# Expert weights in a new host layout, and one expert's load moved into the tile of h

## The chip, the core and the metric

The kernel runs on one core of a Trainium2 chip. The core has five engines with queues of their own: TensorE (PE, with its weight loads shown as PEld), VectorE (DVE), ScalarE (ACT), GpSimd (POOL) and SyncE (SP, which here only issues transfers). Sixteen DMA engines move data between the device memory and the on-chip memory (SBUF, 128 partitions). The metric is the device time of one execution in microseconds (us).

## The reference, cut to what matters

Two layers for 256 tokens of 1,024 features: sparse attention, then a mixture of experts, then a gated embedding. The change lies in the mixture of experts, which runs once in each layer:

```python
def hier_moe(xn, w_group, b_group, w_expert, b_expert, w_gate, w_up, w_down):
    g_prob = softmax(xt @ w_group + b_group)                 # 4 groups, one is taken
    e_logits = (xt @ w_expert + b_expert)                    # 8 experts in the taken group
    ...                                                      # the best two, with their weights
    cw = ...                                                 # [token, 32 experts], two entries per token
    hid = silu(einsum('td,edf->tef', xt, w_gate)) * einsum('td,edf->tef', xt, w_up)
    y = einsum('tef,efd->td', hid * cw[:, :, None], w_down)
```

Here xn is the residual h, normed, with the gain ln_ffn; w_gate and w_up are [2 layers, 32 experts, 1024, 128], w_down is [2, 32, 128, 1024], all in float32.

## The kernel before

The program is written as a straight line of operations on tiles. A planner orders each engine's instructions at build time by its own costs and due times, puts the waits in, and keeps a ring of 102 KB per partition for streamed weights beside a few big named tiles (XA, XB, X2, XH, X3, X4, X5) that are used again and again. SP issues its transfers strictly in its order.

In one mixture of experts, `moe(l, ...)`, the steps are these.

- The last part of the attention output is added to h. The tile of h, [128 tokens, 2 halves, 1024], is XH in the first layer and XA in the second.
- For each half t of the tokens, `transposed(t)` transposes h on PE in eight blocks of 128 features, `logits(t, half)` makes the router's logits with `wr`, `split_h(t)` (line 995, ACT) copies h rounded into `h_hi`, `choose(t)` finds group and experts with a row of small DVE instructions, and `rest_h(t)` (line 998, DVE) writes h minus `h_hi` into `h_lo`. All of these read h through `columns(t)`, which takes feature 8p + k as row p of block k, so neighbours in a block lie 8 elements apart.
- `order(t)` counts each token's place in its expert's list of at most 32 slots; line 986 makes the rank, line 976 (`place`) the one-hot matrix `Gs`. `gather_first` (line 1017) and `gather` (line 1064) multiply `h_hi` and `h_lo` with `Gs`, so that each expert's tokens stand in columns; lines 1088 and 1090 bring them to SBUF with the gain.
- Experts are taken four at a time, in groups j = 0 to 7. `gate_up(j)` (line 1225) runs 64 matmuls on four tiles of weights, `down(j)` (lines 1256 to 1263) the second matrix and the sum into the tokens. `hidden(j)` lies between them.
- `load_wgu(j)` loads gate and up of the four experts, each by two transfers of 512 KB with 4 KB per partition. Groups 0 and 3 use four big tiles, the others the ring. The fourth tile is the one that holds h. `load_wd(j)` loads down. The program calls `load_wgu(0)`, `load_wgu(1)`, `load_wd(0)` after the routing, then `load_wgu(j + 2)` and `load_wd(j + 1)` at group j.
- At group 4 `unsplit_h` (line 1003, DVE) puts h together again from `h_hi` and `h_lo`, through `columns(t)`, into the other of the tiles XA and XH. A ninth, gathered expert (`load_extra`, `rows_of`) covers one list that is longer than 32.

The router's constants come once, in `late_constants`, by seven transfers of the POOL queue during the first attention; line 283 multiplies the gain into `wr`.

Of the kernel before, what the change touches and what calls it, by code (L numbers as in the profile page):

```python
# [18 lines left out]
P = 128  # L19
S = 256  # L20
D = 1024
NT = S // P
NK = D // P
H = 16
HD = 64
NE = 32
NG = 4
# [12 lines left out]
def hybrid_kernel(ctx: ExitStack, tc: tile.TileContext, I: dict, out: bass.AP, dbg=None):  # L40
    nc = tc.nc
# [11 lines left out]
    def nm(s):  # L53
        uid[0] += 1
        return f"{s}_{uid[0]}"
# [7 lines left out]
    def bt(tag, shape, dt=F32):  # L63

        return big.tile(shape, dt, tag=tag, name=nm(tag))

    def wt(tag, shape, dt=F32, bufs=None):
        return wk.tile(shape, dt, tag=tag, name=nm(tag), bufs=bufs)
# [41 lines left out]
    hh = [bt("XH", [P, NT, D])]  # L110
# [45 lines left out]
    rows = wt("hT", [P, P])[0:78]  # L156
# [3 lines left out]
    for r0, src in ((48, I["a_k_norm"][0]), (51, I["a_q_norm"]), (52, I["b_q_norm"]), (53, I["k_norm_shared"][None, :])):  # L160
        n = src.shape[0]
# [41 lines left out]
    for c in range(8):  # L203
        for b in range(2):
            v = SLOPE[8 * (c // 4) + 4 * b + c % 4]
# [38 lines left out]
    g_ffn = cp.tile([P, 2, NK], F32, name="g_ffn")  # L244
    wr = cp.tile([P, 2, NK, NE + NG], F32, name="wr")
    rb = cp.tile([P, 2, NE + NG], F32, name="rb")

    def late_constants():
        nc.gpsimd.dma_start(g_ffn, I["ln_ffn"].rearrange("l (p k) -> p l k", k=NK))
        for l in range(2):  # L250
            nc.gpsimd.dma_start(wr[:, l, :, 0:NE], I["moe_w_expert"][l].rearrange("(p k) e -> p k e", k=NK))
            nc.gpsimd.dma_start(wr[:, l, :, NE:NE + NG], I["moe_w_group"][l].rearrange("(p k) e -> p k e", k=NK))
        nc.gpsimd.dma_start(rb[:, :, 0:NE], I["moe_b_expert"].partition_broadcast(P))
        nc.gpsimd.dma_start(rb[:, :, NE:NE + NG], I["moe_b_group"].partition_broadcast(P))


    iota_e = cp.tile([P, NE], F32, name="iota_e")
# [30 lines left out]

    def columns(t):

        return hh[0][:, t, :].rearrange("q (p k) -> q k p", k=NK)

    def inv_rms(t, ss, rstd):
        junk = wt("sq", [P, D], BF16)
# [577 lines left out]
    def moe(l, out_proj_tail, prefetch):  # L872
# [4 lines left out]
        def load_wgu(j):  # L877
            wgus[j] = []
            for i in range(4):
                e = 4 * j + i  # L880
                gu = [I[src][l, e].rearrange("(p k) f -> p k f", k=NK) for src in ("moe_w_gate", "moe_w_up")]
                if j in (0, 3):
                    w = bt((("XB", "XA", "X2", "XH"), ("XB", "X2", "XH", "XA"))[l][i], [P, 2, NK, P])
                else:
                    w = ring.tile([P, 2, NK, P], F32, name=nm("wgu"))
                for x in range(2):
                    nc.sync.dma_start(w[:, x], gu[x])
                wgus[j].append([w[:, :, k, :] for k in range(NK)])

        def load_wd(j):  # L890
# [41 lines left out]
        def transposed(t):  # L932
            ts_ = slice(t * P, (t + 1) * P)
            inv_rms(t, ss, rstd)
            for k0 in range(0, NK, 4):
                pt = pa([P, 4, P])
                for k in range(4):
                    i = nc.tensor.transpose(pt[:, k, :], columns(t)[:, k0 + k, :], ident)
                if k0:
                    c = nc.scalar.copy(hT[:, k0:k0 + 4, ts_], pt)  # L940
                else:
                    nc.vector.tensor_copy(hT[:, k0:k0 + 4, ts_], pt)
            return i, c
# [3 lines left out]
        def logits(t, half):  # L947
            ts_ = slice(t * P, (t + 1) * P)
            if half == 0:
                pls[t] = pa([P, NE + NG])  # L950
            for k in range(4 * half, 4 * half + 4):
                i = nc.tensor.matmul(pls[t], hT[:, k, ts_], wr[:, l, k, :], start=(k == 0), stop=(k == NK - 1))
            if half == 1:
                nc.vector.scalar_tensor_tensor(lg[:, t, 0:NE + NG], pls[t], rstd[:, t:t + 1], rb[:, l, :], ALU.mult,
                                               ALU.add)
            return i
# [68 lines left out]
        add, i = out_proj_tail(1, 1)  # L1025
        with tc.issue_after(i.ins):
            i = logits(0, 0)
        with tc.issue_after(c.ins):
            split_h(0)
        with tc.issue_after(i.ins):  # L1030
            i, c = transposed(1)
        with tc.issue_after(i.ins):
            i = logits(0, 1)
# [4 lines left out]
        with tc.issue_after(i.ins):  # L1038
            for k in range(2):
                i = logits(1, k)  # L1040
        pg.append(pb([P, 2, 256]))
        with tc.issue_after(i.ins):
            i = keep_warm(pg[0], 4)
        with tc.issue_after(i.ins):
            order(0)
            for k0 in (0, 2):
                i = gather_first(0, k0)
        dump(f"h{1 + 3 * l}", hh[0])
        choose(1)
        with tc.issue_after(i.ins):  # L1050
            i = order(1)
        with tc.issue_after(i.ins):
            for k0 in (4, 6):
                i = gather_first(0, k0)
# [107 lines left out]
        stokx = st("stokx", [CAP, 1], bufs=1)  # L1162
        srsx = st("srsx", [CAP, 1], bufs=1)

        def rows_of(src, o):
            rows = I[src].rearrange("l e d f -> (l e d f)").rearrange("(r n) -> r n", n=D)
            nc.gpsimd.memset(o, 0.0)
            nc.gpsimd.indirect_dma_start(out=o, out_offset=None, in_=rows,
                                         in_offset=bass.IndirectOffsetOnAxis(ap=rowi[:, 0:1], axis=0),
                                         bounds_check=2 * NE * P - 1, oob_is_err=False)  # L1170
# [65 lines left out]

        def load_extra():
            wx.append(bt("X2", [P, 2, D]))
            for x, src in enumerate(("moe_w_gate", "moe_w_up")):
                rows_of(src, wx[0][:, x, :])  # L1240
            wx.append(bt("XB", [P, D]))
            rows_of("moe_w_down", wx[1])

        def hidden(j):
            m = P if j < 8 else CAP
# [35 lines left out]
        def leftover():  # L1281

            cwo = st("oh", [P, NT, NE], bufs=1)
            rs2 = st("rs2", [P, NT], bufs=1)
            nc.vector.tensor_tensor(rs2, rstd, rstd, ALU.mult)
            for t in range(NT):
                nc.vector.tensor_tensor(cwo[:, t], rank[:, t], thr, ALU.is_gt)
            nc.vector.tensor_tensor(cwo, cwo, cw, ALU.mult)
            nc.vector.tensor_tensor(cwo, cwo, rs2[:, :, None].to_broadcast([P, NT, NE]), ALU.mult)
            with tc.For_i(0, rv):  # L1290
                ox = st("ox", [P, 8], bufs=1)
                oi = st("oi", [P, 8], U32, bufs=1)
                nc.vector.max(ox, over)
                nc.vector.max_index(oi, ox, over)
                oif = st("oif", [P, 1], bufs=1)
                nc.vector.tensor_copy(oif, oi[:, 0:1])
                sel = st("sel", [P, NE], bufs=1)
                nc.vector.tensor_scalar(sel, iota_e, oif, None, ALU.is_equal)
                nc.vector.tensor_tensor(over, over, sel, ALU.subtract)
                e = nc.sync.value_load(oi[0:1, 0:1], min_val=0, max_val=NE - 1)  # L1300
                ow = bt("X4", [P, 2, NK, P])
                od = bt("XB", [P, D])
                for x, w in enumerate(("moe_w_gate", "moe_w_up")):
                    nc.sync.dma_start(ow[:, x], I[w][l, bass.ds(e, 1)].rearrange("o (p k) f -> p (o k) f", k=NK))
                nc.sync.dma_start(od, I["moe_w_down"][l, bass.ds(e, 1)].rearrange("o f d -> f (o d)"))
                for t in range(NT):
                    sc_ = st("sc_", [P, NE], bufs=1)
                    cc = st("cc", [P, 1])
                    nc.vector.tensor_tensor(sc_, cwo[:, t], sel, ALU.mult)
                    nc.vector.tensor_reduce(cc, sc_, AX.X, ALU.add)  # L1310
                    gu = banks[0].rearrange("p (x s) -> p x s", x=4)
                    pt = banks[1].rearrange("p (k s) -> p k s", k=4)
                    for k0 in range(0, NK, 4):
                        xT = wt("p1", [P, 4, P], bufs=4)
                        for k in range(4):
                            nc.tensor.transpose(pt[:, k, :], columns(t)[:, k0 + k, :], ident)
                        nc.vector.tensor_tensor(xT, pt, gf[:, k0:k0 + 4, None].to_broadcast([P, 4, P]), ALU.mult)
                        for k in range(4):
                            nc.tensor.matmul(gu[:, 0:2], xT[:, k, :], ow[:, :, k0 + k, :],
                                             start=(k0 + k == 0), stop=(k0 + k == NK - 1))  # L1320
                    hid = silu_mul(gu[:, 0, :], gu[:, 1, :], rstd[:, t:t + 1], cc)
                    nc.tensor.transpose(gu[:, 2, :], hid, ident)
                    hT = wt("hT", [P, P])
                    nc.vector.tensor_copy(hT, gu[:, 2, :])
                    for n in range(2):
                        nc.tensor.matmul(y[t][n], hT, od[:, n * 512:(n + 1) * 512], start=False, stop=False)

        wx = []
# [7 lines left out]
        for j in range(8):  # L1336
# [10 lines left out]
            if j < 7:  # L1347
# [7 lines left out]
                if j in (0, 2, 4):  # L1355
                    i = j // 2 + 1
# [128 lines left out]
    def after_b(c):  # L1485
# [6 lines left out]
    ple(B_p, X)  # L1492


_INS = ['x', 'p', 'ln_mix', 'ln_ffn', 'ln_ple', 'a_w_in', 'a_q_norm', 'a_k_norm', 'a_ck_pos', 'a_ck_w1', 'a_ck_w2',
        'a_cv_pos', 'a_cv_w1', 'a_cv_w2', 'a_w_out', 'kv_norm', 'w_kv_shared', 'k_norm_shared', 'b_w_q', 'b_q_norm',
        'b_w_out', 'moe_w_group', 'moe_b_group', 'moe_w_expert', 'moe_b_expert', 'moe_w_gate', 'moe_w_up',
# [1 line left out]


# [17 lines left out]
```

## Time and profile before

| | us |
|---|---|
| median of 3 runs | 552.87 (551.81 to 553.31) |
| profiled execution | 552.15 |
| its span, first to last instruction | 550.5 |
| PE busy in the span | 523.7 (95%) |
| DVE busy | 351.9 (64%) |
| ACT busy | 282.8 (51%) |
| POOL busy | 57.9 (11%) |

The span is what the trace shows; 1.65 us of the profiled execution lie around it. PE is busy nearly always, so a row that says how long PE stood still and what ended it is worth more here than a row on another engine. [...]

### The profile page before, as it was taken

How to read it: one execution, taken by the hardware profiler on the slowest of the kernel's cores; microseconds unless marked ns; L12 is line 12 of the kernel's file. 1: busy time of each engine (PE TensorE's matmuls, PEld its weight loads, DVE VectorE, ACT ScalarE, POOL GpSimd, SP SyncE). 2: the span in 40 equal slices, each digit the busy share in tenths (PEclk: the TensorE clock that was granted, in tenths of full speed). 3: DMA queues.
4: the chain of work that ended last, by engine and by line, in shares of the span. 5: the costliest groups of instructions: out<-in, count | busy, mean ns of one | idle time of the engine just before them, and what ended most of it. 6: DMA issues, size and time to landing. Idle time of an engine off the chain costs nothing. (4 is left out here: it accounts for less than half of the span.)

```text
span 550.5 us, 10449 instructions
## 1 busy us (share of the span) xinstructions
PE 523.7 (95%) x3804; PEld 373.5 (68%) x3804; DVE 351.9 (64%) x1072; ACT 282.8 (51%) x652; POOL 57.9 (11%) x128
## 2 busy tenths in 40 slices
PE   6999999999897999999999999999987999999996
PEld 6979996677567765464568999656556755555376
DVE  5869979988757645323278986767657535232484
ACT  6759468975526142222379956754352412222391
POOL 5000614213320003100000000000000013000000
PEclk9999999999999899999999999999998999999999
DMA  8986980255778499999972679944672999999702
GB/s 324 356 323 223 189 206 1 86 190 205 299 241 302 176 417 408 391 402 409 387 244 78 208 192 216 405 160 199 224 265 106 402 411 413 410 408 395 272 2 77
DMA packets 52940, 146.14 MB, mean 265 GB/s; under 512 B 5293, under 2 KB 10277, under 8 KB 52885
## 3 DMA queue, kind: packets, MB, share of 16 engines
q1 hardware_dynamic: 51669, 143.38, 72.4%
q0 software_dynamic: 1184, 2.05, 1.4%
q8 instruction: 31, 0.51, 0.4%
q14 instruction: 24, 0.20, 0.1%
q10 hardware_dynamic: 32, 0.01, 0.0%
HBM read 145.94 MB, written 1.05 MB: 267 GB/s over the span
## 5 line engine op out<-in xcount | busy, mean ns | idle before, releaser
L1225 PE MATMUL pb<-wgu,X 128*32 128x256 f32 x768 | 50.4, 380 | 1.0 <-DVE sinf L1150 0.4
L461 ACT ACTIVATE p<-p,mx 128x128 f32<-128x128 f32 (+1 forms) x96 | 42.5, 446 | 9.4 <-DVE mx L459 9.4
L865 ACT ACTIVATE p<-pb,srs 128x128 f32<-128x128 f32 x16 | 5.9, 368 | 80.5 <-PE pb L1225 71.0
L1225 PEld LDWEIGHTS pb<-wgu,X 128*32 128x32 f32 x768 | 29.7, 110 | 17.7 <-issue 2.2
L1270 PE MATMUL pb<-wd,hT 128*32 128x512 f32 x224 | 41.4, 596 | 0.0
L370 DVE TENSOR_TENSOR pta<-pb,p 128x512 fp32r<-128x512 f32 (+1 forms) x36 | 24.8, 690 | 24.0 <-ACT p L370 22.5
L370 ACT CAST p<-pb 128x512 fp32r<-128x512 f32 (+1 forms) x36 | 21.1, 585 | 34.7 <-PE pb L1270 33.2
L381 PE MATMUL pa<-XA,wsp 128*128 128x256 f32 x128 | 37.4, 292 | 0.0
L382 PE MATMUL pa<-XB,wsp 128*128 128x256 f32 x128 | 36.3, 284 | 0.0
L383 PE MATMUL pa<-XA,wsp 128*128 128x256 f32 x128 | 35.9, 282 | 0.0
L868 DVE TENSOR_TENSOR p<-pb,ptb 128x128 f32<-128x128 f32 (+1 forms) x18 | 5.2, 290 | 44.1 <-ACT ptb L867 41.8
L459 DVE CUSTOM_DVE_ANT_0 p<-pb,d_q 128x128 f32<-128x128 f32 (+1 forms) x96 | 29.6, 350 | 4.5 <-PE pb L442 3.4
L490 ACT COPY pta<-pa 128x512 f32<-128x512 f32 (+1 forms) x32 | 14.6, 478 | 34.0 <-PE pa L486 33.8
L472 POOL TENSOR_SCALAR p<-p,cf 128x128 f32<-128x128 f32 x32 | 24.8, 783 | 62.8 <-ACT p L461 29.0
L146 DVE SCALAR_TENSOR_TENSOR wsp<-raw,cols,wsp 128x512 fp32r<-128x512 f32 x40 | 28.0, 747 | 3.4 <-ACT wsp L145 3.3
L571 PE MATMUL pa<-wo,XH 128*128 128x512 f32 x64 | 29.4, 602 | 0.0
L1064 PE MATMUL pb<-rs,X 128*128 128x256 f32 (+1 forms) x192 | 27.1, 293 | 2.0 <-DVE X L1090 2.0
L1064 PEld LDWEIGHTS pb<-rs,X 128*128 128x128 f32 x192 | 24.3, 188 | 5.7 <-DVE X L1090 2.6
L1263 PE MATMUL pa<-p,rrow 128*128 128x512 f32 (+1 forms) x72 | 27.3, 424 | 0.0
L1263 PE MATMUL pa<-pta,rrow 128*128 128x512 f32 (+1 forms) x72 | 26.7, 420 | 0.4 <-DVE pta L370 0.4
L142 DVE SCALAR_TENSOR_TENSOR wsp<-raw,g_mix,wsp 128x256 fp32r<-128x256 f32 x64 | 26.5, 475 | 0.0
L145 ACT ACTIVATE wsp<-raw,cols 128x512 fp32r<-128x512 f32 x40 | 26.2, 717 | 0.0
(385 smaller groups left out, 1464.9 us busy)
## 6 DMA issues: line engine op xcount, KB each, us to landing
wgu<-in_moe_w_gate_dram SPq DMA_DIRECT2D x48, 512.0 KB, 6.5
wgu<-in_moe_w_up_dram SPq DMA_DIRECT2D x48, 512.0 KB, 10.2
wd<-in_moe_w_down_dram SPq DMA_DIRECT2D x48, 512.0 KB, 8.8
raw<-in_a_w_in_dram SPq DMA_DIRECT2D x16, 512.0 KB, 6.0
raw<-in_ple_w_gate_dram SPq DMA_DIRECT2D x16, 512.0 KB, 8.3
wd<-in_moe_w_down_dram SPq DMA_DIRECT2D x16, 256.0 KB, 6.2
wo<-in_a_w_out_dram SPq DMA_DIRECT2D x8, 512.0 KB, 8.4
raw<-in_b_w_q_dram SPq DMA_DIRECT2D x8, 512.0 KB, 4.4
```

The lines of the kernel that those rows point to most:

```text
L146: nc.vector.scalar_tensor_tensor(lo, src, g, hi.bitcast(F32), ALU.mult, ALU.subtract)
L370: return nc.scalar.copy(hi, src), eng.tensor_tensor(lo, src, hi.bitcast(F32), ALU.subtract)
L381: nc.tensor.matmul(o, a[0], b[0], start=first, stop=False)
L382: nc.tensor.matmul(o, a[0], b[1], start=False, stop=False)
L383: return nc.tensor.matmul(o, a[1], b[0], start=False, stop=last)
L459: nc.vector.tensor_tensor_reduce(pt_[:, br, :], st_[:, br, :], dt_, -SLOPE[hh], 3e38, ALU.add, ALU.min, accum_out=mx[:, t, br:br + 1])
L461: mark["exp", c] = nc.scalar.activation(pt_[:, br, :], pt_[:, br, :], AF.Exp, bias=mx[:, t, br:br + 1], scale=-1.0, accum_out=sums[:, t, b ...
L571: m = nc.tensor.matmul(pt, self.oT[0][:, 2 * j + i, t * P:(t + 1) * P], self.raw[j][:, i, n * 512:(n + 1) * 512], start=(i == 0), stop=(i ...
L1064: nc.tensor.matmul(pt, part_columns(x, t)[:, k, :], Gs[i][:, t, 0:e1], start=(t == x == 0), stop=(t == x == 1))
L1225: last_ = nc.tensor.matmul(gu[32 * i:32 * i + 32, 0:2], xg[:, k, 32 * i:32 * i + 32], wgu[i][k], start=(k == 0), stop=(k == NK - 1), tile_ ...
L1263: nc.tensor.matmul(y[t][n], gt[0:m, t * P:(t + 1) * P], ysx[x][0:m], start=(first and x == 0), stop=(final and x == 1))
L1270: nc.tensor.matmul(ysp[32 * i:32 * i + 32, :], hT[:, 32 * i:32 * i + 32], wd[i][n], start=True, stop=True, tile_position=(0, 32 * i))
```

## The change

The host now lays out four inputs before the launch. Gate and up of an expert become one array in which a partition holds its 2 x 8 x 128 values in one run of 8 KB; the order of the features is k * 128 + p for row p of block k. Router weights (experts and groups in one array), router bias and the gain ln_ffn follow the same order. `columns(t)` therefore reads and writes 128 neighbours. A transfer of 1 MB takes the place of two of 512 KB, and three POOL transfers the place of seven. The gathered ninth expert needs one indirect transfer for gate and up where it had two. And in `load_wgu` the fourth expert of group 0 goes to the ring, while the fourth expert of group 1 takes the tile of h.

```diff
 def late_constants():
-    nc.gpsimd.dma_start(g_ffn, I["ln_ffn"].rearrange("l (p k) -> p l k", k=NK))
-    for l in range(2):
-        nc.gpsimd.dma_start(wr[:, l, :, 0:NE], I["moe_w_expert"][l].rearrange("(p k) e -> p k e", k=NK))
-        nc.gpsimd.dma_start(wr[:, l, :, NE:NE + NG], I["moe_w_group"][l].rearrange("(p k) e -> p k e", k=NK))
-    nc.gpsimd.dma_start(rb[:, :, 0:NE], I["moe_b_expert"].partition_broadcast(P))
-    nc.gpsimd.dma_start(rb[:, :, NE:NE + NG], I["moe_b_group"].partition_broadcast(P))
+    nc.gpsimd.dma_start(g_ffn, I["g_ffn"])
+    nc.gpsimd.dma_start(wr, I["router"])
+    nc.gpsimd.dma_start(rb, I["router_b"].partition_broadcast(P))
...
-    return hh[0][:, t, :].rearrange("q (p k) -> q k p", k=NK)
+    return hh[0][:, t, :].rearrange("q (k p) -> q k p", k=NK)
...
             e = 4 * j + i
-            gu = [I[src][l, e].rearrange("(p k) f -> p k f", k=NK) for src in ("moe_w_gate", "moe_w_up")]
-            if j in (0, 3):
+            if j == 3 or (j == 0 and i < 3) or (j == 1 and i == 3):
                 w = bt((("XB", "XA", "X2", "XH"), ("XB", "X2", "XH", "XA"))[l][i], [P, 2, NK, P])
             else:
                 w = ring.tile([P, 2, NK, P], F32, name=nm("wgu"))
-            for x in range(2):
-                nc.sync.dma_start(w[:, x], gu[x])
+            nc.sync.dma_start(w, I["moe_gu"][l, e])
...
-        for x, src in enumerate(("moe_w_gate", "moe_w_up")):
-            rows_of(src, wx[0][:, x, :])
+        rows_of(I["moe_gu"].rearrange("l e p x k f -> (l e p) (x k f)"), wx[0].rearrange("p x d -> p (x d)"))
...
+def _layout(inputs):
...
+    def parts(w):
+        w = w.reshape(*w.shape[:-2], NK, P, w.shape[-1])
+        return np.moveaxis(w, -3, -2)
+    gate, up = a.pop("moe_w_gate"), a.pop("moe_w_up")
+    a["moe_gu"] = np.stack([parts(gate), parts(up)], axis=-3)
+    a["router"] = np.moveaxis(parts(np.concatenate([a.pop("moe_w_expert"), a.pop("moe_w_group")], axis=-1)), 0, 1)
+    a["router_b"] = np.concatenate([a.pop("moe_b_expert"), a.pop("moe_b_group")], axis=-1)
+    a["g_ffn"] = np.moveaxis(a.pop("ln_ffn").reshape(2, NK, P), 2, 0)
```

## Rows read from the trace of the kernel before

**Rows 1.** The page's list of engines: busy us, share of the span, instructions.

```profile
PE 523.7 (95%) x3804; PEld 373.5 (68%) x3804; DVE 351.9 (64%) x1072; ACT 282.8 (51%) x652; POOL 57.9 (11%) x128
```

**Rows 2.** Waits of PE, whole span: us in total, times, longest us.

```profile
PE pb L1017 <- DVE rs L976: 4.7, 2, 2.5
...
PE pb L1064 <- DVE X L1090: 2.0, 3, 0.8
PE pa L485 <- POOL p L472: 1.6, 1, 1.6
PE pb L1225 <- DMA XA<-in_moe_w_up_dram: 1.5, 1, 1.5
PE pb L1017 <- DVE es L1112: 1.4, 2, 0.7
PE pb L1147 <- DVE X L1090: 0.9, 2, 0.5
```

**Rows 3.** Timeline of PE, both layers: start, us, [idle before <- releaser].

```profile
175.90 1.22 PE L1017 MATMUL pb<-rs,X 128*128 128x256 f32 x8 [2.47 <-DVE rs L976]
...
180.36 3.75 PE L1017 MATMUL pb<-rs,X 128*128 128x256 f32 x16 [0.72 <-DVE es L1112]
...
413.23 2.08 PE L1017 MATMUL pb<-rs,X 128*128 128x256 f32 x8 [2.24 <-DVE rs L976]
...
417.76 2.13 PE L1017 MATMUL pb<-rs,X 128*128 128x256 f32 x16 [0.71 <-DVE es L1112]
...
422.00 0.38 PE L1225 MATMUL pb<-XA,X 128*32 128x256 f32 x1 [1.54 <-DMA XA<-in_moe_w_up_dram]
...
426.40 3.78 PE L1225 MATMUL pb<-wgu,X 128*32 128x256 f32 x64 [0.20 <-DVE sinf L1150]
```

**Rows 4.** Timeline of DVE, first layer, routing and group 4.

```profile
173.04 0.26 DVE L954 SCALAR_TENSOR_TENSOR lg<-pa,rstd,rb 128x36 f32<-128x36 f32 x1 [0.27 <-ACT rstd L297]
...
173.29 1.98 DVE L998 TENSOR_TENSOR X<-XH,X 128x1024 fp32r<-128x1024 f32 x1
...
177.56 2.04 DVE L998 TENSOR_TENSOR X<-XH,X 128x1024 fp32r<-128x1024 f32 x1
...
214.65 2.20 DVE L1003 TENSOR_TENSOR XA<-X,X 128x1024 f32<-128x1024 f32 x1 [3.22 <-PE pb L1225]
...
216.88 0.69 DVE L1090 TENSOR_TENSOR X<-pb,g_ffn 128x512 f32<-128x512 f32 x1
...
217.88 2.14 DVE L1003 TENSOR_TENSOR XA<-X,X 128x1024 f32<-128x1024 f32 x1
```

**Rows 5.** Timeline of SP, its transfers: start of issue, us.

```profile
105.47 2.59 SPq L887 DMA_DIRECT2D wgu<-in_moe_w_gate_dram  x2
...
179.75 0.33 SPq L887 DMA_DIRECT2D XH<-in_moe_w_gate_dram  x1
...
187.87 0.34 SPq L887 DMA_DIRECT2D XB<-in_moe_w_gate_dram  x1
...
417.10 0.33 SPq L887 DMA_DIRECT2D XA<-in_moe_w_gate_dram  x1
```

**Rows 6.** Stretches: PE, PEld, DVE, ACT, POOL busy, granted clock, DMA share, GB/s.

```profile
178.00:180.00 2.00, 1.64 (x9) 1.43 (x8) 2.00 (x5) 0.80 (x1) 0.00 (x0) 0.50 0.01 2
...
417.00:418.00 1.00, 0.29 (x4) 0.27 (x3) 1.00 (x7) 0.00 (x0) 0.00 (x0) 1.00 0.00 0
...
188.00:285.00 97.00, 94.24 (x813) 53.80 (x813) 40.55 (x122) 30.30 (x66) 7.42 (x8) 1.00 0.99 385
```

**Rows 7.** Groups by line and shape: busy us, mean ns of one.

```profile
L370 DVE TENSOR_TENSOR wsp<-wo,wsp 128x512 fp32r<-128x512 f32 x16 | 10.8, 696 | 0.0
...
L295 ACT ACTIVATE sq<-XH 128x1024 bf16<-128x1024 f32 x6 | 6.3, 1052 | 3.1 <-DVE XH L574 3.1
...
L868 DVE TENSOR_TENSOR p<-pb,ptb 128x128 f32<-128x128 f32 x16 | 4.7, 292 | 37.3 <-ACT ptb L867 35.0 <-PE pb L1064 2.2
```

**Rows 8.** Timeline of ACT, first layer, the second copy of h.

```profile
170.85 2.05 ACT L995 CAST X<-XH 128x1024 fp32r<-128x1024 f32 x1
```

More of the change, by code (lines that the diff above doesn't have):

```diff
@@ L1163, in moe, with rows_of @@
         srsx = st("srsx", [CAP, 1], bufs=1)
-        def rows_of(src, o):
-            rows = I[src].rearrange("l e d f -> (l e d f)").rearrange("(r n) -> r n", n=D)
+        def rows_of(rows, o):
             nc.gpsimd.memset(o, 0.0)
@@ L1238, in load_extra @@
             wx.append(bt("X2", [P, 2, D]))
-            for x, src in enumerate(("moe_w_gate", "moe_w_up")):
-                rows_of(src, wx[0][:, x, :])
+            rows_of(I["moe_gu"].rearrange("l e p x k f -> (l e p) (x k f)"), wx[0].rearrange("p x d -> p (x d)"))
             wx.append(bt("XB", [P, D]))
-            rows_of("moe_w_down", wx[1])
+            rows_of(I["moe_w_down"].rearrange("l e f d -> (l e f) d"), wx[1])
         def hidden(j):
@@ L1302, in leftover @@
                 od = bt("XB", [P, D])
-                for x, w in enumerate(("moe_w_gate", "moe_w_up")):
-                    nc.sync.dma_start(ow[:, x], I[w][l, bass.ds(e, 1)].rearrange("o (p k) f -> p (o k) f", k=NK))
+                nc.sync.dma_start(ow.rearrange("p x k f -> p (x k f)"),
+                                  I["moe_gu"][l, bass.ds(e, 1)].rearrange("o p x k f -> p (o x k f)"))
                 nc.sync.dma_start(od, I["moe_w_down"][l, bass.ds(e, 1)].rearrange("o f d -> f (o d)"))
@@ L1492, in hybrid_kernel @@
     ple(B_p, X)
+def _layout(inputs):
+    import numpy as np
+    a = {n: np.asarray(inputs[n]) for n in _INS}
+    def parts(w):
[6 more added lines that the diff above has]
+    a["g_ffn"] = np.moveaxis(a.pop("ln_ffn").reshape(2, NK, P), 2, 0)
+    return {n: np.ascontiguousarray(v) for n, v in a.items()}
 _INS = ['x', 'p', 'ln_mix', 'ln_ffn', 'ln_ple', 'a_w_in', 'a_q_norm', 'a_k_norm', 'a_ck_pos', 'a_ck_w1', 'a_ck_w2',
@@ L1501 @@
 def kernel(**inputs):
-    import numpy as _np
     import concourse.bacc as _bacc
@@ L1508 @@
     arrays, aps = {}, {}
-    for name in _INS:
-        a = _np.ascontiguousarray(inputs[name])
+    for name, a in _layout(inputs).items():
         arrays[f"in_{name}_dram"] = a
```

## The prediction, made before the change was run

> **What bounds the kernel now.** I read the list of engines first. PE is busy for 523.7 of 550.5 us and no other engine comes near [rows 1], so time is won only where PE stands still or runs at its low clock. The list of PE's waits comes next [rows 2]. Five of the entries shown lie in the two mixtures of experts, in operations that the change touches: 4.7 and 1.4 us at line 1017 (the first gather waits for the one-hot matrix), 2.0 us at line 1064 and 0.9 us at line 1147 (the third gather waits for line 1090, which empties its PSUM), and 1.5 us at line 1225, the one long wait for a transfer. The timeline of PE tells where these stand [rows 3]: 2.47 and 0.72 us in the first layer's routing, 2.24 and 0.71 us in the second's, and 1.54 us in the second layer's first `gate_up`.
>
> The timeline of DVE gives the reason for the first two kinds [rows 4]. `rest_h` (line 998) takes 1.98 and 2.04 us, and the rank and the one-hot matrix for which PE waits are queued behind it. `unsplit_h` (line 1003) takes 2.20 and 2.14 us, and line 1090 at 216.88 starts just as it ends. Both go through `columns(t)`, 8 elements apart. The transfer is the fourth expert's: its tile is h's own, so SP issues it at 417.10, when `rest_h(1)` has read h [rows 5], and PE gets it at 422.00 [rows 3].
>
> [...]
>
> **The change part by part.** *DVE, a row of 1,024 neighbours.* No such instruction with two inputs is in the trace. The nearest with all operands in SBUF are 512 elements at 0.696 us and 128 at 0.292 us [rows 7]: 1.05 ns an element, so 1.23 us for 1,024. The bounds are 0.70 us (the 512 row) and 1.98 us (no gain at all). I take 1.23, since the line through both rows needs no more than their slope.
>
> *Routing, first layer.* DVE's row from 173.29 to PE's restart at 180.36 has no idle entry of note, so what `rest_h` gives up is given on: 0.75 and 0.81 us. The second copy of h on ACT (2.05 us from 170.85, [rows 8]) stands ahead of the rstd for which DVE waits 0.27 us at 173.04 [rows 4]. A row of 1,024 neighbours on ACT takes 1.05 us [rows 7], a microsecond less, and the 0.27 us go. Together 1.83 us. What is late next is still the chain of small DVE instructions: of the gap of 2.47 us some 1.45 stay.
>
> *Routing, second layer.* The same 0.75 and 0.81 us, with no wait for rstd. Here PE can become the later one: restarted at 412.48, with twice eight matmuls at up to 2.08 us each (the slow ones of 413.23, [rows 3]), it could be free for the last 16 only at 416.64, while DVE would be ready at 416.20. So between 1.1 and 1.56 us; I take 1.4, because the second eight need not all be slow.
>
> *The clock in the first layer.* Between nothing and 3.75 - 2.13 = 1.62 us. In the second layer a standstill of 2.24 us also led to the low clock (eight matmuls in 2.08 us instead of 1.22), but it was back at 1.00 at 417 to 418 [rows 3, 6]. The standstill that stays, 1.45 us, is below both, and nearest to the two of 1.6 and 1.54 us at lines 485 and 1225 [rows 2, 3]; `gate_up` goes on at 422.00 with matmuls of 0.38 us, the full clock's duration. So I take the whole 1.62 us, as the nearest rows have it, and keep nothing as the other end. [...]
>
> *The fourth expert.* In group 0 it goes to the ring, where loads run far ahead (the first at 105.47, [rows 5]); the ring's first eight expert slots stay eight, since group 1 gives one up. The wait of 1.54 us in the second layer goes. In the first layer the same load lands just before its use; it would have become the next wait once the gather is faster, and does not. The load into h's tile is now group 1's. SP can issue it when `rest_h(1)` ends, near 415.5 in the second layer, and as 417.10 to 422.00 was 4.9 us, it lands near 420.4. `gate_up(1)` stands at 426.40 [rows 3] and would come some 4.5 us sooner at most, at 421.9: 1.5 us of cover, and more in the first layer. Group 3's fourth load then waits for `gate_up(1)` instead of `gate_up(0)`. Three transfers of 1 MB are ahead of it, at 385 GB/s [rows 6] 2.7 us each, 8.2 us in all, longer than the 3.78 us of `gate_up(1)` and the gap ahead of it. So the DMA engines don't run dry. What is queued behind it on SP is group 4, for which no slot was free earlier.
>
> *`unsplit_h`.* Line 1064 waits 2.0 us in three times, the longest 0.8; two of 0.8 follow line 1003, and the rest, 0.4, lies elsewhere. Line 1147 waits 0.9 us in two times [rows 2]. With 1.23 us the first `unsplit_h` ends at 215.9, line 868 (0.29 us) follows, and line 1090 is through by 216.8, when PE wants it; the second ends 0.9 us sooner, more than the wait of 0.5. Of 2.5 us I count 2.4; nothing if the price of a row stays.
>
> *Nothing for the rest.* From 188 to 285 us the DMA engines are busy 0.99 of the time at 385 GB/s and PE still 94.24 of 97 us [rows 6], so fewer and longer transfers have at most 2.8 us to win in a layer, and `unsplit_h` accounts for 1.3 of it. The list of waits names no other long one for a transfer [rows 2]. SP's 64 fewer issues of 0.33 us [rows 5] are not waited for. The POOL transfers lie in the first attention, over 100 us ahead of the router, and the indirect ones three groups ahead of the ninth expert. PE's transposes of h read the new order without a change of shape; I count them the same.
>
> **The sum**: 1.83 + 1.4 + 1.62 + 1.54 + 2.4 = 8.8 us. The profiled execution of 552.15 becomes 543.4; the median of the runs is 0.7 above it, so 544.1. PE stays the bound, so no later stage takes it back.
>
> **The rivals.** *The clock falls again.* For it: both layers show a fall after a standstill. Against it: the standstill is 40% shorter. Without its term the time is 545.7; if it also catches the second layer's last 16 matmuls, which come 1.4 us sooner, 547.3.
>
> *The planner moves something.* 64 transfers fewer change its costs, and so perhaps orders far from here; the fourth expert's load could also come late in the ring. For it: the order is the planner's. Against it: the ring holds as much as before. Losing the 1.54 us, or giving back 2 to 4 us elsewhere, 545.6 to 548.
>
> *The layout does not do what it says*: a row of 1,024 takes 2 us however its elements lie. Against it is the slope of [rows 7]. Then only 0.27 and 1.54 us are won: 551.1.
>
> *Slower: the load into h's tile stands behind group 3's on SP.* SP serves its waits in order. Now the load into h's tile is issued at 179.75, 8 us ahead of group 3's first at 187.87 [rows 5]. Placed behind group 3's three, which wait for `gate_up(0)`, it would land four transfers, 10.9 us, after that, while `gate_up(1)` wants it within about 1 us: some 10 us in each layer, 564. It decides from a landing 4.4 us late in each layer. Against it: it is free sooner and earlier in the program. [...]
>
> **How the numbers follow.** Forecast 0.45, its own range 543.0 to 545.4 (the bounds of the second layer's routing, and parts of the clock's term). Clock 0.25. Planner 0.15. Layout 0.05. Slower 0.05. A gain that the planner's order gives back whole 0.05. The range of 542.5 to 548.0 takes in the first three and leaves out 0.15, and some of the planner's. A change of 0.3% (1.7 us) is about what this kernel's runs can tell from none. Faster: 0.45 + 0.25 + 0.15 + 0.03 of the layout rival, which ends at that bound: 0.88; same 0.07; slower 0.05.
>
> **What the profile after would show.** Lines 998 and 1003 near 1.23 us and 995 near 1.05. The gaps at line 1017 near 1.45 us and below 0.4. No wait at line 1225 for the fourth expert; its load in the ring long before the routing, h's tile loaded for group 1 right after `rest_h(1)`. Line 1064 without its waits of 0.8 us. The last 16 gather matmuls of the first layer in 2.1 us. The prediction is wrong if the rows of 1,024 stay near 2 us, if `gate_up(1)` waits for its fourth tile, or if PE gains new gaps in the attentions.

## The result: 550.37 us, a quarter of the gain that was forecast

The changed kernel takes 550.37 us (median of 19 runs, 545.10 to 552.45), the kernel before on the same chip 552.68 (551.61 to 553.82): a ratio of 0.9948, 95% interval 0.9928 to 0.9968. It is faster, by 2.3 us of the 8.6 forecast (552.7 to 544.1), and its median lies 2.4 us above the upper end of the range. New is the spread: the kernel before stays within 2.2 us, the runs of the changed one lie up to 7.35 us apart. The profiled execution took 547.75 us, with a span of 546.1. One execution of the run e8_shift, 732.95 us at a mean clock of 0.653 (clocks are the granted share of PE's full one), was slow throughout and is in none of the figures below.

The list of PE's waits after the change answers to [rows 2]. The columns are us in total, times, longest us.

```profile
PE pb L1013 <- DVE rs L972: 3.1, 2, 1.6
PE pb L1220 <- issue: 2.2, 1, 2.2
...
PE pb L1013 <- DVE es L1108: 1.5, 2, 0.8
...
PE pb L1226 <- DMA X<-in_moe_gu_dram,rowi: 0.8, 1, 0.8
...
PE pb L1060 <- DVE X L1086: 0.3, 1, 0.3
```

Lines have moved by four to six: 1013 was 1017, 1060 was 1064, 1220 was 1225. The gather's wait is down from 4.7 to 3.1 us, the third gather's waits of 2.0 and 0.9 have shrunk to 0.3, and the fourth expert's 1.5 is gone. Two entries are new: 2.2 us of "issue", in which PE waited for nothing that the list names, and 0.8 us in the second layer for the load of the ninth, gathered expert (line 1226).

PE's timeline, with the rows that answer to [rows 3], shows both the gain and its loss.

```profile
169.39 1.07 PE L934 MATMUL pa<-ident,XH 128*128 128x128 f32 x8
...
175.48 2.08 PE L1013 MATMUL pb<-rs,X 128*128 128x256 f32 x8 [1.51 <-DVE rs L972]
...
179.94 2.13 PE L1013 MATMUL pb<-rs,X 128*128 128x256 f32 x16 [0.71 <-DVE es L1108]
...
408.21 1.21 PE L1013 MATMUL pb<-rs,X 128*128 128x256 f32 x8 [1.59 <-DVE rs L972]
...
411.84 2.13 PE L1013 MATMUL pb<-rs,X 128*128 128x256 f32 x16 [0.77 <-DVE es L1108]
...
493.92 3.18 PE L1220 MATMUL pb<-wgu,X 128*32 128x256 f32 x50 [0.30 <-DMA wd<-in_moe_w_down_dram]
499.29 1.38 PE L1220 MATMUL pb<-wgu,X 128*32 128x256 f32 x11 [2.20 <-issue]
...
503.69 0.33 PE L1250 MATMUL pb<-ident,p 128*128 128x128 f32 x1
```

The same two places in the kernel before, `gate_up(7)` of the second layer and the first transpose behind it:

```profile
502.62 3.78 PE L1225 MATMUL pb<-wgu,X 128*32 128x256 f32 x62 [0.30 <-PEq L1344]
...
508.14 0.33 PE L1256 MATMUL pb<-ident,p 128*128 128x128 f32 x1
```

At `gate_up(7)` the changed kernel leads by 502.62 - 493.92 = 8.70 us, against a sum of 8.8 in the prediction. At the next transpose the lead is 508.14 - 503.69 = 4.45 us, which is what is left at the end (550.5 - 546.1 = 4.4). In between stands the 2.20 us of "issue", fifty matmuls behind the branch that skips the block of `leftover()` (`tc.If`, line 1338), and then a slow clock. The stretches after the change, columns as in [rows 6], show it, and the first layer's routing above it:

```profile
176.00:177.00 1.00, 1.00 (x7) 1.00 (x6) 0.97 (x8) 0.14 (x1) 0.39 (x3) 0.50 0.90 369
...
410.00:412.00 2.00, 1.23 (x10) 1.12 (x11) 2.00 (x7) 1.10 (x1) 0.00 (x0) 1.00 0.00 0
...
498.00:500.00 2.00, 0.71 (x9) 0.46 (x12) 0.00 (x0) 0.00 (x0) 0.00 (x0) 0.87 1.05 384
500.00:502.00 2.00, 2.00 (x17) 1.02 (x12) 0.20 (x1) 0.84 (x3) 0.00 (x0) 0.50 1.05 388
```

So in this execution the clock fell in the first layer's routing and behind the stop, and stayed up in the second layer's routing. DVE did as forecast:

```profile
173.44 1.22 DVE L994 TENSOR_TENSOR X<-XH,X 128x1024 fp32r<-128x1024 f32 x1
...
L999 DVE TENSOR_TENSOR XA<-X,X x2: 1216/1220/1224, 212.0 to 214.4; 128x1024 f32<-128x1024 f32 x2
```

Two questions follow: what the stop is, and what sets the time of the runs that are slower than this one.

### The profile page after: what moved, and what is told of

The parts are those of the page before. It is cut to its first block, busy times and chain, and to the rows that moved or that the text cites. A ratio compares the mean times of both kernels' runs of the same rounds, so it can differ in the third digit from the quotient of the medians.

```text
span 546.1 us, 10308 instructions
## 1 busy us (share of the span) xinstructions
PE 520.7 (95%) x3804; PEld 366.1 (67%) x3804; DVE 346.6 (63%) x1072; ACT 278.9 (51%) x652; POOL 50.5 (9%) x120
## 3 DMA queue, kind: packets, MB, share of 16 engines
q0 software_dynamic: 784, 2.05, 1.0%
HBM read 145.94 MB, written 1.05 MB: 269 GB/s over the span
## 4 chain that ended last, share of the span: by engine, by line
PE 39%; DMA 6%; issue 2%; DVE 2%; ACT 1%; POOLq 0%; POOL 0%; DVEq 0%; ACTq 0%; SPq 0%
PE pa L568 5%; PE pb L1220 5%; PE pa L378 4%; PE pa L380 4%; PE pa L379 3%; PE pb L1264 3%; PE pa L1257 2%; DMA wgu<-in_moe_gu_dram 2%; DMA X<-in_moe_gu_dram,rowi 2%; DMA wd<-in_moe_w_down_dram 2%; PE pb L380 1%; PE pb L379 1%; PE pb L378 1%; PE pa L610 1%; PE pa L500 1%
## 5 line engine op out<-in xcount | busy, mean ns | idle before, releaser
L1220 PE MATMUL pb<-wgu,X 128*32 128x256 f32 x768 | 58.2, 385 | 3.1 <-issue 2.2
L1264 PE MATMUL pb<-wd,hT 128*32 128x512 f32 x224 | 42.8, 612 | 0.3 <-DVE cws L1147 0.2
```

What stands on the lines that cost most here:

```text
L1220: last_ = nc.tensor.matmul(gu[32 * i:32 * i + 32, 0:2], xg[:, k, 32 * i:32 * i + 32], wgu[i][k], start=(k == 0), stop=(k == NK - 1), tile_ ...
L1264: nc.tensor.matmul(ysp[32 * i:32 * i + 32, :], hT[:, 32 * i:32 * i + 32], wd[i][n], start=True, stop=True, tile_position=(0, 32 * i))
```

## The experiments

**The same kernel again, and the shape of the transfers.** The first run repeats the kernel without an edit. The second keeps 1 MB in one transfer but with rows of 4 KB; the third cuts it in two again, of the new array.

```
 e2_rows4k:  -  nc.sync.dma_start(w, I["moe_gu"][l, e])
             +  nc.sync.dma_start(w, I["moe_xp"][l, e].rearrange("x p k f -> p x k f"))
 e3_halves:  +  for x in range(2):
             +      nc.sync.dma_start(w[:, x], I["moe_gu"][l, e][:, x])
```

> The changed kernel once more, for a second profile and more runs. Every theory expects about 550 us, between 545 and 552.5. In a run that is slower than the profiled one of 547.75 us, the code theory (PE waits for its own instructions while the DMA engines move rows of 8 KB, and the clock falls after it) expects more gaps of PE of 1 to 3 us with no releaser inside the expert groups of either layer, each with a stretch at clock 0.50 behind it. The routing theory (the clock falls again after the standstill in the routing) expects the low stretches at the first gathers instead.

> One transfer of 1 MB an expert as in the change, but from an array in which gate and up lie apart, so that a partition's run is 4 KB. Code theory with the length of a run as its cause: 543.5 to 546 us with a small spread, no gaps without a releaser in the expert groups. Transfer-size theory (more bytes queued by each issue): as the change, about 550. Order theory (the planner's new order is to blame): about 550. Branch theory (only the code behind the skipped block is late): about 550.

> The change's layout, loaded by two transfers of 512 KB an expert, with runs of 4 KB. Code theory with the length of a run: 543.5 to 546 us. Transfer-size theory: 543.5 to 546 us as well. Order theory: about 550 unless the planner's order changes back. Branch theory: about 550.

e1_again: 547.36 us (545.17 to 551.77, 9 runs), ratio 0.9914 (0.9885 to 0.9942). e2_rows4k: 548.58 (544.32 to 550.01), 0.9915 (0.9885 to 0.9944). e3_halves: 545.41 (543.93 to 550.73), 0.9873 (0.9846 to 0.9899). The profiles of the first two show the stop at the same place, that of the third does not. e1_again's is of one of its longer executions, 550.94 us, and has the same single stop; its clock is low in both layers (about 174 to 186 and 410 to 414 us), as the routing theory expected. e3_halves's is of its slowest execution, 550.73 us: without a stop, the clock is at 0.50 in both routings. PE's timeline of e1_again, e2_rows4k, e3_halves:

```profile
497.16 3.18 PE L1220 MATMUL pb<-wgu,X 128*32 128x256 f32 x50 [0.30 <-PEq L1338]
502.54 1.50 PE L1220 MATMUL pb<-wgu,X 128*32 128x256 f32 x11 [2.20 <-issue]
```

```profile
496.36 3.18 PE L1220 MATMUL pb<-wgu,X 128*32 128x256 f32 x50 [0.30 <-PEq L1338]
501.73 0.85 PE L1220 MATMUL pb<-wgu,X 128*32 128x256 f32 x11 [2.19 <-issue]
```

```profile
500.69 3.78 PE L1221 MATMUL pb<-wgu,X 128*32 128x256 f32 x62 [0.30 <-PEq L1339]
```

The length of a row is not the cause of the stop. In e2_rows4k's profile the clock does not fall behind it (eleven matmuls in 0.85 us). PE's instructions stand in the same order in the kernel before, the changed one and all three of these, so their order isn't either. The median of the change itself moved by 3 us between two sets of runs.

**The branch.** The block behind `tc.If`, which is skipped with these inputs, is left out with its branch.

```
 e4_nobranch:  -  banks = [pb([P, 512]) for _ in range(2)]
               -  rv = nc.values_load(noveri[0:1, 0:1], min_val=0, max_val=NE)
               -  with tc.If(rv > 0):
               -      leftover()
```

> The change without the conditional block for further long lists (which these inputs never enter) and without the read of its count. Branch theory: 543 to 546 us, no gap without a releaser in the last groups. Code theory: some gaps go, as there is less code to bring, but runs of 8 KB still hold it up elsewhere: 547 to 550. Order and transfer-size theories: about 549 to 550, less only what the block itself costs (0.3 us of PE a layer).

546.76 us (545.61 to 547.66), 0.9896 (0.9877 to 0.9915), and no stop. That is still above the 543 to 546 that the branch theory gave: the routing's slow stretches are there as before.

**The clock.** Matmuls on a constant that nothing reads fill PE's waits in the routing; e6_nobranch_warm has them on e4_nobranch. e8_shift, run beside them, moves the code and leaves the clock alone; e7_layout is told below.

```
 e5_warm:    i = order(0)
          +  i = keep_warm(pg[0], 6)          # 1.5 us wait
             for k0 in (0, 2): i = gather_first(0, k0)
             ...
             for k0 in (4, 6): i = gather_first(0, k0)
          +  keep_warm(pa([P, 2, 256]), 3)    # 0.7 us wait
 e8_shift: +  for _ in range(64):             # at the start of the program
           +      nc.tensor.matmul(pt[:, 0, 0:1], ones, ones[:, 0:1], start=True, stop=True)
```

> The changed kernel with six 512-column matmuls on a constant in the 1.5 us wait before the first gathers and three in the 0.7 us wait before the last sixteen, in both layers; nothing reads them. Clock theory (a stop of 1.5 us still takes the clock down in some runs and layers, for 4 to 11 us each, and that is what the runs of one kernel differ by): both low stretches behind the routing are gone, sixteen gathers take 2.1 us in each layer, the mean clock is 0.993 or more in all runs, the runs lie within 2 us, and the median is near the fastest runs of the changed kernel, 544 to 546, depending on whether the 2.2 us stop behind the branch stays. Rival (the runs differ by the transfers, and the clock only follows the waits): runs between 545 and 552 as before, median 547 to 550. Second rival (the added matmuls are in the way): the gathers start later than now after the placing, and the median is 0.5 to 2 us above the changed kernel's.

> Without the skipped block and its branch, and with the matmuls of e5_warm. If the branch stop (2.2 us and the slow clock behind it) and the clock behind the routing are the two places where the forecast gain went, and they are independent, this run has neither: 542 to 544, runs within 2 us, mean clock 0.995 or more, so at least 2 us below e4_nobranch (546.76). If the clock is not what set e4_nobranch's time: 545.5 to 547.7 as there.

> The changed kernel with 64 one-column matmuls (128 instructions with their weight loads) put at the very start, where the engine waits for the first input until 3.8 us; nothing else moves. Code theory (the 2.2 us stop after fifty matmuls of the second layer's seventh group comes from where the instructions lie): the stop is gone from there, or stands after a different number of matmuls, and if it is gone the time falls by 2 to 4.4 us at an equal routing clock. Rival (the stop comes from the order of work around it, the data or the tiles): it stays 2.2 us long after the same fifty matmuls.

e5_warm: 543.13 us (542.93 to 544.65), 0.9833 (0.9818 to 0.9847). e6_nobranch_warm: 542.33 (541.46 to 543.23), 0.9810 (0.9796 to 0.9825), 4.4 us below e4_nobranch. Their mean clocks are 0.996 to 1.000, and neither profile has a stop. e8_shift: 547.66 (546.98 to 550.35, five executions), 0.9922 (0.9901 to 0.9942). Its stop is gone, but its clock is 0.981 to 0.987. The routing of the first layer on PE, in e5_warm and then in e8_shift:

```profile
175.46 1.46 PE L177 MATMUL pb<-ones 128*128 128x512 bf16 x6
177.12 1.21 PE L1013 MATMUL pb<-rs,X 128*128 128x256 f32 x8 [0.20 <-DVE rs L972]
...
178.76 1.20 PE L1013 MATMUL pb<-rs,X 128*128 128x256 f32 x8
179.80 0.82 PE L177 MATMUL pa<-ones 128*128 128x512 bf16 x3
180.71 2.13 PE L1013 MATMUL pb<-rs,X 128*128 128x256 f32 x16
```

```profile
175.39 2.08 PE L1016 MATMUL pb<-rs,X 128*128 128x256 f32 x8 [1.51 <-DVE rs L975]
...
177.44 2.05 PE L1016 MATMUL pb<-rs,X 128*128 128x256 f32 x8
180.25 3.75 PE L1016 MATMUL pb<-rs,X 128*128 128x256 f32 x16 [0.71 <-DVE es L1111]
```

The same work takes 1.21, 1.20 and 2.13 us in the one and 2.08, 2.05 and 3.75 in the other: behind the standstill of 1.51 us the clock is at 0.50. In e8_shift's profile the clock is 0.50 from 175 to 185 us and low again from 410 to 414. Without the stop, the clock costs 547.66 - 543.13 = 4.5 us. One program also had its low stretches in different places and for different times: the changed kernel's first profile has one of 3.4 us, in the first layer (175.2 to 178.6), that of e1_again some 10 us in the first and 3.4 in the second. What decides between them is not shown.

What is left of low clock in e5_warm lies in the first attention. There PE stands still for 1.57 us in every profile whose trace is at hand (seventeen, all but e9_warm_shift256's), at line 485 of the kernel before (482 in the changed one), one of the two rows that the prediction held to be nearest. The stretch behind it in the kernel before, and then in e5_warm:

```profile
150.00:152.00 2.00, 1.31 (x14) 0.93 (x14) 2.00 (x11) 1.69 (x6) 0.01 (x1) 1.00 0.92 326
```

```profile
150.00:152.00 2.00, 2.00 (x7) 1.48 (x6) 0.84 (x3) 2.00 (x9) 0.61 (x2) 0.50 0.51 213
```

The clock fell behind this one standstill in seven of the seventeen, and not in the other ten.

**Where the code lies.** e9_warm_shift256 puts 110 one-column matmuls ahead of e5_warm, e11_warm_first leaves out the three matmuls of e5_warm's second wait. A matmul here is two instructions, its weight load and itself (the profile of the changed kernel has 3,804 of each).

```
 e9:   e5_warm, and e8_shift's loop with range(110)
 e11:  e5_warm without  keep_warm(pa([P, 2, 256]), 3)
```

> e5_warm (543.13) with 110 one-column matmuls (220 instructions) at the start; with the 36 instructions that e5_warm itself puts ahead of the second layer's branch, the code behind the branch lies 256 instructions further than in the changed kernel, where it stopped for 2.2 us, against 36 in e5_warm and 128 in e8_shift, where it did not. Code theory (the stop depends on where the code lies in blocks of 256 instructions): the stop of about 2.2 us after fifty matmuls of gate_up(7) is back, and with the clock steady elsewhere this prices it: 545 to 547.5, of which up to 0.6 is the later start. Rival (any shift removes it): no stop, 543 to 544.

> e5_warm with only the six matmuls in the 1.5 us wait, none in the 0.7 us wait. If the longer wait alone takes the clock down: as e5_warm, 543 to 545, runs within 2 us (plus 2 to 4 us if the stop behind the branch is back at this place of the code). If the wait of 0.7 us counts too: low stretches begin at the last sixteen gathers in some runs, and the runs spread up to 548.

e9_warm_shift256: 550.71 us (545.69 to 553.82, 12 runs), 0.9948 (0.9923 to 0.9973). The stop is back after fifty matmuls, and there is one in the first layer too, which puts the time above the 545 to 547.5 expected. e11_warm_first: 545.64 (543.23 to 549.20), 0.9861 (0.9831 to 0.9891); its six runs are three of 543.23 to 544.29 and three of 546.99 to 549.20, and in the profile of the slowest of these the stop stands after 38. The timelines, of e9_warm_shift256 (both layers) and of e11_warm_first:

```profile
260.79 2.36 PE L1228 MATMUL pb<-wgu,X 128*32 128x256 f32 x38 [0.35 <-PEq L1346]
266.48 2.39 PE L1228 MATMUL pb<-wgu,X 128*32 128x256 f32 x25 [3.33 <-issue]
...
498.69 3.18 PE L1228 MATMUL pb<-wgu,X 128*32 128x256 f32 x50 [0.30 <-PEq L1346]
504.06 0.85 PE L1228 MATMUL pb<-wgu,X 128*32 128x256 f32 x11 [2.20 <-issue]
```

```profile
494.88 2.36 PE L1223 MATMUL pb<-wgu,X 128*32 128x256 f32 x38 [0.30 <-PEq L1341]
500.25 2.19 PE L1223 MATMUL pb<-wgu,X 128*32 128x256 f32 x25 [3.01 <-issue]
```

e11_warm_first has twelve matmuls, 24 instructions, more ahead of that place than the changed kernel, and its stop comes twelve matmuls sooner; 256 instructions more bring it back to fifty. So the stop is tied to a place in the code, and the two shifts fit one that repeats every 256 instructions. PE's stop does not stand right behind the branch but 38 or 50 matmuls further on. The 0.7 us wait alone leaves the clock up in e11_warm_first's profile (sixteen gathers in 2.13 and 2.14 us); in the mixtures its clock is low only behind the stop.

**Whose transfers.** The kernel before and e3_halves have the same instructions of PE at the same places, and no stop in their profiles. e13_shift256_halves is e9_warm_shift256 with two transfers for each expert, e14_before_warm_shift256 is the kernel before with a steady clock and the code at that place, e10_before_warm the same without the shift.

```
 e10_before_warm:  keep_warm(pg[0], 10) and keep_warm(pa([P, 2, 256]), 3), placed as in e5_warm
 e13_shift256_halves:       e9_warm_shift256 and the two lines of e3_halves
 e14_before_warm_shift256:  e10_before_warm and e8_shift's loop with range(102)
```

> The kernel before with ten 512-column matmuls on a constant in its 2.47 and 2.24 us wait before the first gathers and three in the 0.7 us wait before the last sixteen. Clock theory: its low stretches at 177 to 185 and 413 to 417 go, as the profile prices them some 2.5 to 4 us: 548.5 to 550.5. Against e5_warm, both with a steady clock, the change is then worth the forecast 8.8 less the clock term of 1.6 that both now have: 6 to 7.5 us. Rival (the changed kernel lost by something that the added matmuls repair in it alone): 552 to 553, unchanged.

> e9_warm_shift256 (550.71, with stops of 3.3 and 2.2 us behind the two branches) with each expert's gate and up as two transfers of 512 KB; TensorE's instructions are the same ones at the same places, SyncE has one issue more for each expert. If the stops need the 1 MB transfers: no stop, 542 to 544. If place alone decides: the stops stay, 547.5 to 551.

> e10_before_warm (552.80, no stop) with 102 one-column matmuls (204 instructions) at the start, which with its own 52 puts the code behind the second layer's branch 256 instructions further than in the kernel before and in the changed one. If place alone decides when the clock is steady: a stop after fifty matmuls of gate_up(7) of the second layer, 2 us or more above e10_before_warm. If the stop belongs to the changed kernel's transfers: no stop, 552.5 to 554.

e13_shift256_halves: 543.14 us (542.91 to 544.45), 0.9827 (0.9814 to 0.9841), with no stop in either layer (the rows below). So the two stops of e9_warm_shift256, with what follows from them, cost 550.71 - 543.14 = 7.6 us, and here it takes the single transfer of 1 MB for them to appear. e14_before_warm_shift256: 553.49 (552.36 to 554.25), 1.0009 (1.0000 to 1.0019), no stop.

```profile
262.30 3.78 PE L1229 MATMUL pb<-wgu,X 128*32 128x256 f32 x62 [0.30 <-PEq L1347]
...
494.16 3.78 PE L1229 MATMUL pb<-wgu,X 128*32 128x256 f32 x62 [0.30 <-DMA wgu<-in_moe_gu_dram]
```

The traces show what comes late. The list of DMA queues has a row for instructions, q8: 31 packets of 16 KB in the changed kernel's whole run, 32 in the runs with 128 to 256 more instructions of PE, so about one for every 256 instructions (7,608 matmuls and weight loads to 31 packets in the changed kernel are 245, with branches and waits not counted). The rows (packets, MB, share of the 16 engines) of the changed kernel from 480 to 496 us, where q8 has no row, then its q8 from 496 to 498 us, and the rows of e13_shift256_halves from 480 to 496 us:

```profile
q1 hardware_dynamic: 1593, 6.55, 101.4%
```

```profile
q8 instruction: 1, 0.02, 3.5%
```

```profile
q1 hardware_dynamic: 1792, 6.53, 102.3%
q8 instruction: 1, 0.02, 0.4%
```

In the changed kernel the packet moves from 496.88 to 497.99 us. PE has run out of its fifty matmuls at 497.10 and goes on at 499.29. Fourteen of the seventeen profiles have the branch, which makes 28 such places. The five with a stop have no packet of q8 in the 12 us ahead of the first matmul behind the branch; the other 23 have one. So what PE waits for in the stop is, by these rows, its next block of instructions, which starts late but does not move slowly: 1.1 us, where the other packets take 0.9 to 2.5.

e10_before_warm missed what I expected: 552.80 us (551.94 to 553.98), 1.0004 (0.9992 to 1.0015). Its clock is 0.996 to 1.000 and its gathers are as quick as e5_warm's, but PE's timeline shows what takes their place:

```profile
184.42 0.38 PE L1230 MATMUL pb<-XH,X 128*32 128x256 f32 x1 [1.53 <-DMA XH<-in_moe_w_up_dram]
...
421.89 0.38 PE L1230 MATMUL pb<-XA,X 128*32 128x256 f32 x1 [1.63 <-DMA XA<-in_moe_w_up_dram]
```

So in the kernel before the slow clock cost nothing in the first layer: the fourth expert, in h's tile, was that late anyway.

**The two parts alone.** e7_layout gives h's tile back to the first group in the changed kernel as it is; e15_layout_alone_steady does so with e5_warm's matmuls and two transfers for each expert; e16_tile_alone_steady is e10_before_warm with the tile moved.

```
 e7, e15:  -  if j == 3 or (j == 0 and i < 3) or (j == 1 and i == 3):
           +  if j in (0, 3):
 e16:      the reverse
```

> The changed kernel with the tile of h given back to the first group's fourth expert, as before: the layout alone. By the working on record the tile's move is worth the 1.54 us wait of the second layer's fourth expert: that wait, 1 to 2 us, is back in gate_up(0) of the second layer, and the time is 1 to 2 us above the changed kernel on the same chip with the same clock. Rival (the wait is only moved to the end of the loads, which are late by then anyway, or was covered): the wait is back and the start of the second layer's last group is as early as in the changed kernel; no difference. Rival (the shift of loads matters elsewhere): faster than the changed kernel.

> The layout alone with the two losses kept out: the changed kernel with the matmuls of e5_warm, two transfers for each expert, and the tile of h given back to the first group's fourth expert. e10_before_warm waited 1.53 and 1.63 us for that expert, e7_layout 1.4 and 1.34. If the tile's move is worth those waits: 2.7 to 3.2 us above e13_shift256_halves (543.14, less some 0.6 for the later start), 545.5 to 546.5, and the layout's share against e10_before_warm (552.80) is some 6.5 us. If the waits are made good later: 542.5 to 543.5.

> The tile's move alone, with a steady clock: e10_before_warm with the tile of h given to an expert of the second group. If it is worth the two waits of 1.53 and 1.63 us there: 549.3 to 550.3. If the layout's earlier freeing of the tile is needed for it, or the first group's other experts land as late: 551.5 to 553.

e7_layout: 551.06 us (548.42 to 553.70, 12 runs), 0.9978 (0.9961 to 0.9994), with a stop of 1.92 us and waits of 1.4 and 1.34 for the fourth expert. Whether that is the 1 to 2 us above the changed kernel that were expected can't be told, as that kernel's own median moved by 3 us. In e7_layout's profile the standstills of 1.51 and 1.59 us are there and the clock stays at 1.00 in both layers, behind the stop too. e15_layout_alone_steady: 549.68 (549.24 to 552.95), 0.9949 (0.9933 to 0.9964). e16_tile_alone_steady: 548.01 (547.64 to 549.57), 0.9919 (0.9904 to 0.9933). The waits of e15_layout_alone_steady for that expert:

```profile
PE pb L1226 <- DMA XH<-in_moe_gu_dram: 2.1, 1, 2.1
PE pb L1226 <- DMA XA<-in_moe_gu_dram: 2.0, 1, 2.0
```

With a steady clock and no stop: neither part 552.80 us, the layout alone 549.68 (-3.1), the tile alone 548.01 (-4.8), both 543.14 (-9.7). Both expectations put the layout's part too high and the tile's too low. The two waits are 4.1 of the 6.5 us that the move is worth beside the layout.

**The fastest version.** e12_halves_nobranch_warm is e6_nobranch_warm with the two lines of e3_halves.

> e6_nobranch_warm (542.33) with each expert's gate and up matrices as two transfers of 512 KB again, of the new layout. If e3_halves was faster than the changed kernel only because it lacked the stop behind the branch, two transfers are worth nothing here, or cost some 64 issues: 541.5 to 543.5. If smaller transfers land sooner by themselves: below 541.5.

541.33 us (540.78 to 542.77), 0.9800 (0.9780 to 0.9821), the lowest of the study. It lies just under the 541.5 below which the expectation took smaller transfers to land sooner by themselves, but five runs don't settle that, as they overlap with e6_nobranch_warm's five (541.46 to 543.23). One wait points that way: the ninth expert of the second layer is waited for 1.56 us in e6_nobranch_warm's profile and 0.34 in this one. This version lacks the skipped block. The one with the block and no stop in its profile is e13_shift256_halves or e5_warm, at 543.1.

## Why the prediction was wrong

**Rows of 1,024.** Right: 1.22 us at lines 994 and 999, 1.04 at 991 on ACT, as the slope of [rows 7] had it.

**Routing.** Right in its size. From the start of the second transposes to the last sixteen gathers the second layer took 11.44 us before (406.32 to 417.76) and 9.80 after (402.04 to 411.84): 1.64 us, for 1.4 in the sum. The first layer gained 11.60 - 10.55 = 1.05 with its low clock and 11.60 - 9.67 = 1.93 in e12_halves_nobranch_warm without it, for 1.83. Only the gaps lie otherwise than I said: the 0.7 us gap stays, and PE reaches it sooner.

**`unsplit_h`.** Right: 2.0 and 0.9 us of waits became 0.3.

**The clock: the first step that failed.** "So I take the whole 1.62 us", which is 3.75 less 2.13 us for the last sixteen gathers of the two layers [rows 3], the first layer's at clock 0.50 [rows 6]: the standstill that stays, 1.51 to 1.59 us, does still take the clock down, in most cases: behind 11 of the 14 in the seven profiles that keep it. The two rows that I held to be nearest, of 1.6 and 1.54 us, told nothing of this place; the first of them is the 1.57 us at line 485, behind which the clock fell in seven later profiles, so its one row was one outcome of two. It was my rival with a chance of 0.25; its 547.3 for both layers is near e8_shift's 547.66, which has the low clock in both and no stop. The price is 4.4 to 4.5 us for both layers, since more than the sixteen gathers runs slow.

**The transfers: the second.** "Nothing for the rest" gave the single 1 MB transfers a value of nothing, with no end on the side of a loss. With them, and with the code at some places, a block of PE's instructions starts to move only behind the branch, and PE stops for 1.9 to 3.3 us, in four of the six profiles with a slow clock behind it (0.50 in the changed kernel's); nothing later makes that good. "PE stays the bound, so no later stage takes it back" was wrong for this reason: the engine that is the bound can also wait for its own instructions. That the block is late is shown by its packets; why it starts late beside single transfers is not shown. The same passage put the indirect loads three groups ahead of the ninth expert and counted nothing for them: in the second layer that expert is waited for 0.7 to 1.7 us in nine of the ten profiles with single transfers, and 0.5 us at most in those with two.

**The fourth expert: a mis-sized term.** The wait of 1.54 us went, and the load of h's tile for the second group was never waited for, as I said. But the wait was only what the slow clock and the slow routing left of it. With these gone the same load is late in both layers, by 2.1 and 2.0 us in e15_layout_alone_steady, and the move is worth 4.8 us alone and 6.5 beside the layout.

**The other rivals.** PE's instructions stand in the order they had, so the planner moved nothing there; the layout does what it says; h's tile is filled in time.

**The sum.** 543.13 (e5_warm) and 543.14 (e13_shift256_halves) are a microsecond below the 544.1 forecast: the mechanisms were there, and a steady clock and fetched instructions were assumed. That they come so close is in part luck. The sum had 7.25 us for the layout with its clock term and 1.54 for the tile; measured they are 3.1 and 4.8 alone, and 1.8 more only together. The changed kernel's median lies 7.2 us above these; the clock costs 4.5 where it falls in both layers, the one stop with the slow clock behind it took 8.70 - 4.45 = 4.25 in the profile, and two stops cost up to 7.6. How often each comes in its 19 runs can't be told, as only profiled executions show a stop. Open stays why the block starts late only beside 1 MB transfers, and why in e5_warm and e8_shift, at other places of the code, it came in time.

## What to carry to other kernels

Here the gain on the bound engine was kept whole only where that engine's clock and instructions held up behind it (543.1 us, against 550.37): fill a standstill of 1.5 us that remains with matmuls that nothing reads (worth 4.4 to 4.5 us here), and look for "issue" gaps behind a skipped block before and after joining transfers, with the row of the instruction queue beside them. A row of the clock behind one standstill is one outcome (behind the 1.57 us at line 485 it fell in seven profiles of seventeen): look at several profiles before leaning on it. A wait hidden by another wait has no row, as the first layer's 2.1 us in e15_layout_alone_steady had none in the kernel before; ask of each wait that goes what would be late if everything ahead of it were faster. When runs of one kernel spread over 7 us where the other's stay within 2, compare versions with the spread removed before apportioning anything.

## What was not expected of the hardware

The stop ends 5.37 us after PE's first matmul behind the branch, whether 38 or 50 matmuls lay between (493.92 to 499.29 in the changed kernel, 498.69 to 504.06, and 494.88 to 500.25 in e11_warm_first). In e7_layout that time is 5.11 us (496.50 to 501.61), and 5.69 in the first layer of e9_warm_shift256 (260.79 to 266.48). In the five traces with a stop the late packet starts 2.8 to 3.0 us after that matmul. Nine matmuls a layer that nothing reads, 2.3 us of PE's time, took up to 4.5 us off the kernel. And thirteen of them a layer, on the kernel before, raised the mean clock of its profile from 0.990 to 1.000 and saved nothing.
